# First feed-forward of a hybrid encoder layer: the first sequence's gate products taken from unnormalised rows, with 1/rms applied afterwards

## The chip, the core and the metric

The kernel runs on one core of a Trainium2 chip. Its engines have queues of their own and run in the order in which their instructions stand: PE (TensorE, matrix products, with its weight loads shown as PEld), DVE (VectorE), ACT (ScalarE), POOL (GpSimd) and SP (SyncE, here the issuer of most DMAs). They wait for each other by semaphores. The metric is the device time of one execution in microseconds (us).

## The reference, cut to what matters

Two sequences of 512 tokens (`x_prompt`, `x_sample`, 1024 channels) go through one encoder layer: a feed-forward, a mixing block and a second feed-forward. The change touches the first feed-forward alone:

```python
def rms_norm(x, g):
    y = xf * lax.rsqrt(jnp.mean(xf * xf, axis=-1, keepdims=True) + EPS)
    return (y * g.astype(jnp.float32)).astype(x.dtype)

def swiglu(x, w_gate, w_up, w_down):
    return (jax.nn.silu(x @ w_gate) * (x @ w_up)) @ w_down

x = x + 0.5 * swiglu(rms_norm(x, ffn1_norm), ffn1_w_gate, ffn1_w_up, ffn1_w_down)
```

All of it is float32; `D_FF` is 2816, so 22 blocks of 128 features.

## The kernel before

Activations lie with channels on the 128 partitions and tokens along the free dimension, so the token rows of the input are first transposed on PE (`turn`, L1236). Each float32 operand is split into a rounded half and a rest (`put`, L278 and L279, for activations; `w_pair`, L291 and L292, for weights), and `product` (L333) makes 12 matmuls of one product: four blocks of 128 channels by three pairings of halves.

Gate and up projections of both sequences are computed together by a scheme with seven products instead of eight (named B11, B21, B22, T1 to T4). B11 and B21 are the two channel halves of the plain gate product of the first sequence: after B11 its partial sum is copied out as `v1` (L341), after B21 the whole is copied out through Silu as `g0` (L348). The other five need sums of both sequences and of gate and up weights. This gives 22 steps, one for each block of features.

For ten of the 22 blocks, the products B11 and B21 are made ahead (`Up.begin`) while the second sequence is still being loaded, normalised and summed; `v1` and `g0` are parked in DRAM (`kept`) and fetched again in `resume` (L467). `Up.rest` then goes through all 22 steps in the order of `ORDER`, which alternates a resumed block (five products) with a fresh one (seven products), and ends on four fresh and two resumed blocks. `gu_rest` is one step: product T2 into bank Y, T1 into Z, T3 on top of Y, B22 on top of Z, T4 on top of Y. Between them DVE reads the banks: L364 adds `v1` and Y and must be done before T3 may write to Y; L372 reads Y before T4, L377 reads Z, L382 reads Y last. The results are split and written to DRAM by `Sides.out` (L396, L397) for the down projection.

At the start, SP issues the loads of the four token blocks of `x_prompt`, one of `x_sample`, the gate weights of block 0, then the rest. `rows_rstd` squares and sums each token row as its block lands and makes 1/rms by eleven small DVE instructions; `turn` transposes all four token blocks for one channel block at a time, each into a bank of its own; `keep_x` copies the turned rows out and stores them; `bcast_psum` (L213) spreads 1/rms over the partitions; `first_x` multiplies the turned rows by the norm weight and 1/rms (`scaled`, L1260) and splits them. Only then can `begin(0)` run. The norm weight `g1` and four small tensors of the mixing block are loaded by POOL's DMA queue, element by element.

A planner orders the instructions of each engine by program order and by the offsets given with `shifted`; `pin` keeps the written order.

Of the kernel before, what the change touches and what calls it, by code (L numbers as in the profile page):

```python
# [26 lines left out]
def encoder(ctx, tc, I, outs):  # L27
# [95 lines left out]
    nc.gpsimd.dma_start(g1, I["ffn1_norm"][0].rearrange("(k p) -> p k", p=P))  # L123


# [4 lines left out]
    pw = PT()[:, 0:P]  # L130
# [150 lines left out]
    def right_sums(xc, k, x0l, x0u, x1l, x1u):  # L281

        V_.tensor_tensor(x0l, x1l, x0l, op=ALU.subtract)
        V_.tensor_tensor(x1l, x1u, x1l, op=ALU.subtract)
        V_.tensor_tensor(x1u, x1u, x0l, op=ALU.subtract)
        V_.tensor_tensor(x0u, x0u, x1u, op=ALU.subtract)
        for i, t in ((T1, x0l), (T2_, x1u), (T3, x1l), (T4, x0u)):
            put(xc[i], k, t)

    def w_pair(t, src, pin=lambda i: i):  # L290
        pin(nc.scalar.activation(t[:, 0], src, AF.Copy))  # L291
        pin(V_.tensor_tensor(t[:, 1], src, f(t[:, 0]), op=ALU.subtract))  # L292
# [11 lines left out]
    def gu_left_a(rg, pin=lambda i: i):  # L304

        wa = w8_tile()
        w_pair(wa, rg.rearrange("p (a k) c -> p a k c", a=2), pin)
        return {B11: part(wa, 0), B21: part(wa, 1)}
# [34 lines left out]

    def gu_first_b(X, W, xc, g0):

        product(X, W[B21], xc[B21], False)
        with shifted(SOONER):
            nc.scalar.activation(g0, X, AF.Silu)  # L348

    def gu_rest(W, xc, got, ring, mid):  # L350
# [75 lines left out]
    class Up:  # L426


        def __init__(self, xc, wg, wu, rb):
            self.xc, self.rb = xc, rb  # L430
# [3 lines left out]
            self.ring.rows["o"] += tables(FFN_ROWS)  # L434
            self.ring.join("x", "v", "h")
# [14 lines left out]
        def begun(self):  # L450
            if self.open:
                j, X, W = self.open
                t = self.ring("k")
                gu_first_b(X, W, self.xc, t)
# [3 lines left out]
        def left(self, j):  # L458
            return gu_left_a(self.fetch(j, (0,))[0])

        def rest(self, raw, at=None, hook=None):
            ring = self.ring

            def resume(j):
                got = ring("v"), ring("h")
                for t, d in zip(got, self.kept.pop(j)):
                    nc.sync.dma_start(t, d)  # L467
                return got
# [5 lines left out]
            for i, j in enumerate(ORDER):  # L474
# [8 lines left out]
                h = gu_rest(W, self.xc, got, ring, lambda: then.append(resume(nxt)) if nxt in self.kept else None)  # L483
# [730 lines left out]
    pin = tc.keep_in_program_order  # L1214
    for _ in range(8):
        pin(nc.tensor.matmul(pw, ones, ones, start=True, stop=True))
# [7 lines left out]
    up = Up(xc, I["ffn1_w_gate"][0], I["ffn1_w_up"][0], rbuf[0])  # L1224
    xins = [I[n][0] for n in ("x_prompt", "x_sample")]

    kept = [[dpool.tile([P, S], F32, name=f"kept{j}_{i}") for i in range(2)] for j in range(AHEAD)]

# [4 lines left out]
    def turn(s, k, bank):  # L1233
        p = bank()
        for b in range(4):
            nc.tensor.transpose(p[:, b * P:(b + 1) * P], raws[s][:, b, k * P:(k + 1) * P], ident)  # L1236
        return p
# [6 lines left out]
    orow = up.ring.rows["o"]  # L1244

    def rows_rstd(s, engines):

        sq = [spool.tile([P, 4], F32, tag="cs4", bufs=4, name=nm("cs4")) for _ in range(2)]
        for b in range(4):
            for i in range(2):  # L1250
                x_, to = raws[s][:, b, i * S:(i + 1) * S], sq[i][:, b:b + 1]
                if engines[i] is V_:
                    V_.scalar_tensor_tensor(orow[3 + i], x_, 1.0, x_, op0=ALU.mult, op1=ALU.mult, accum_out=to)
                else:
                    nc.scalar.activation(orow[3 + i], x_, AF.Square, accum_out=to)
        V_.tensor_tensor(sq[0], sq[0], sq[1], op=ALU.add)
        return rstd_cols(sq[0], 4, D)
# [5 lines left out]
    raw0 = up.fetch(0, (0,), raws[0][:, 1, 0:1])  # L1263
    load_x(1)
    raw1 = [up.fetch(j, (0,))[0] for j in (1, 2)]
    x0 = up.ring.rows["x"]
    x0r = orow[:2] + up.ring.rows["s"] + orow[5:7] + orow[2:3]
    rs = rows_rstd(0, (V_, nc.scalar))
    for k, bank in enumerate((MM, PS, PT, MM, PS, PT, MM, PO)):
        keep_x(0, k, turn(0, k, bank), x0r[k])  # L1270
    W = [gu_left_a(raw0[0])]
    with shifted(-60):
        R0 = bcast_psum(rs)
# [6 lines left out]
    for k in range(HK_):  # L1280
        first_x(k)
    up.begin(0, W[0])
    W.append(gu_left_a(raw1[0]))
    for k in range(HK_, KD):
        first_x(k)
# [3 lines left out]
    rs = rows_rstd(1, (nc.scalar, nc.scalar))  # L1289
    raw0 += up.fetch(0, (1,))  # L1290
# [5 lines left out]
    for k in range(HK_):  # L1296
        x1l, x1u = x1[2 * k % 4], x1[(2 * k + 1) % 4]
        for t, kk, bank, kr in ((x1l, k, PS, orow[3]), (x1u, k + HK_, PT, orow[4])):
            p = turn(1, kk, bank)
# [220 lines left out]
```

## Time and profile before

| | |
|---|---|
| median of 3 runs | 2083.98 us (2081.9 to 2084.88) |
| the profiled execution's own time | 2082.11 us |
| its span, first to last instruction | 2080.3 us |
| granted clock of TensorE, mean | 0.997 |
| PE busy | 2060.4 us (99%) |
| DVE busy | 1551.1 us (75%) |
| ACT busy | 894.6 us (43%) |
| POOL busy | 97.7 us (5%) |

The profile has a page with busy times, a strip of 40 slices, queues and the costliest groups, and views of the trace: a timeline by engine (start, length, engine, line, operation, tile written and tiles read, count, and in brackets the idle time before and what ended it), groups by line, waits, and tables by stretch (length, busy time and count of PE, PEld, DVE, ACT and POOL, then the granted clock, the busy share of the DMA engines and GB/s). Consecutive instructions of a kind stand merged in one row, with their count. DVE and ACT instructions overlap a little at their ends, so that the distance between two starts is less than the length of one.

### The profile page before, as it was taken

To read this page: it belongs to the slowest core of one execution; us is meant where nothing else is said; L and a number is where in the kernel's file an instruction comes from. 1 tells how busy PE (TensorE), PEld (TensorE's weight loads), DVE (VectorE), ACT (ScalarE), POOL (GpSimd) and SP (SyncE) were. 2 spreads that over 40 slices of the span, in tenths; PEclk is the share of its full clock that TensorE was granted. 3 is DMA by queue.
4 is the path that set the end of the run, shared out by engine and by line. 5 is a ranking of instruction groups with operands and counts; after the bars stand their busy time and mean duration, and the time that the engine had idled before them with its cause. 6 is when DMAs were issued, how large, how long until landed. Compare 5 with 4: busy or idle time off the path is not lost.

```text
span 2080.3 us, 27215 instructions
## 1 busy us (share of the span) xinstructions
PE 2060.4 (99%) x9478; PEld 1691.4 (81%) x9478; DVE 1551.1 (75%) x2836; ACT 894.6 (43%) x1645; POOL 97.7 (5%) x114
## 2 busy tenths in 40 slices
PE   8999999999999999999999999999999999999998
PEld 6888888888888877888878788888888888888887
DVE  7888888786797897575567646555788888786797
ACT  6544444443234566463345443324444444442222
POOL 1000000001003000100120000002000000000000
PEclk9999999999999999999999999999999999999999
DMA  9655655599766655777684345677656555599753
GB/s 280 203 173 194 193 171 182 200 342 362 262 222 243 218 152 174 265 240 268 210 286 160 107 149 190 208 255 245 200 177 200 192 172 182 187 348 347 270 189 116
DMA packets 307065, 454.33 MB, mean 218 GB/s; under 512 B 20064, under 2 KB 178864, under 8 KB 305904
## 3 DMA queue, kind: packets, MB, share of 16 engines
q1 hardware_dynamic: 305056, 447.13, 63.6%
q0 software_dynamic: 1872, 5.46, 0.8%
q8 instruction: 75, 1.23, 0.2%
q14 instruction: 62, 0.51, 0.1%
HBM read 285.63 MB, written 166.89 MB: 218 GB/s over the span
## 4 chain that ended last, share of the span: by engine, by line
PE 95%; DVE 3%; DMA 1%; ACT 1%; issue 0%; SPq 0%; DVEq 0%; ACTq 0%
PE mm L755 20%; PE pss L333 17%; PE pst L333 11%; PE mm L333 10%; PE mm L589 9%; PE pst L589 4%; PE pss L589 4%; PE mm L739 4%; PE pso L589 3%; PE pso L1029 1%; PE pss L1002 1%; PE pso L739 1%; PE pst L1021 1%; PE pso L1165 1%; PE pst L755 1%; PE pss L755 1%
## 5 line engine op out<-in xcount | busy, mean ns | idle before, releaser
L755 PE MATMUL mm<-xh,w 128*128 128x512 f32 x896 | 290.4, 394 | 0.0
L333 PE MATMUL pss<-xc,w 128*128 128x512 f32 x1056 | 256.2, 391 | 0.6 <-DVE t L364 0.6
L333 PE MATMUL mm<-xc,w 128*128 128x512 f32 x1056 | 253.4, 391 | 2.0 <-DVE w L292 0.7
L333 PE MATMUL pst<-xc,w 128*128 128x512 f32 x1056 | 253.6, 389 | 0.0
L333 PEld LDWEIGHTS pss<-xc,w 128*128 128x128 f32 x1056 | 196.9, 188 | 47.8 <-DVE t L364 7.2
L333 PEld LDWEIGHTS mm<-xc,w 128*128 128x128 f32 x1056 | 197.3, 188 | 45.2 <-DVE w L292 1.4
L333 PEld LDWEIGHTS pst<-xc,w 128*128 128x128 f32 x1056 | 198.2, 188 | 41.2
L755 PEld LDWEIGHTS mm<-xh,w 128*128 128x128 f32 x896 | 167.7, 188 | 33.5
L589 PE MATMUL mm<-rt,w 128*128 128x512 f32 (+1 forms) x819 | 188.4, 384 | 0.0
L755 PE MATMUL mm<-xl,w 128*128 128x512 f32 x448 | 176.2, 393 | 0.0
L589 PEld LDWEIGHTS mm<-rt,w 128*128 128x128 f32 x819 | 151.3, 188 | 29.8
L291 ACT ACTIVATE w<-t 128x512 fp32r<-128x512 f32 x176 | 106.9, 627 | 139.0 <-issue 55.2
L292 DVE TENSOR_TENSOR w<-t,w 128x512 fp32r<-128x512 f32 x176 | 118.3, 689 | 54.9 <-ACT w L291 52.9
L333 PE MATMUL pss<-xc,f 128*128 128x512 f32 x528 | 126.8, 389 | 0.0
L333 PEld LDWEIGHTS pss<-xc,f 128*128 128x128 f32 x528 | 99.1, 188 | 20.6
L657 ACT ACTIVATE w<-wr 128x512 fp32r<-128x512 f32 x72 | 45.1, 632 | 138.2 <-PE pso L589 70.8
L657 ACT ACTIVATE w<-t 128x512 fp32r<-128x512 f32 x82 | 51.8, 632 | 107.4 <-PE pst L589 62.4
L755 PEld LDWEIGHTS mm<-xl,w 128*128 128x128 f32 x448 | 84.2, 188 | 16.6
L589 PE MATMUL pss<-rt,w 128*128 128x512 f32 x396 | 93.7, 389 | 0.0
L589 PE MATMUL pst<-rt,w 128*128 128x512 f32 x396 | 93.7, 389 | 0.0
L239 ACT ACTIVATE w<-wr 128x1024 fp32r<-128x1024 f32 (+1 forms) x56 | 57.3, 1028 | 73.7 <-PE mm L755 30.2
L589 PEld LDWEIGHTS pss<-rt,w 128*128 128x128 f32 x396 | 74.3, 188 | 15.4
(343 smaller groups left out, 3641.6 us busy)
## 6 DMA issues: line engine op xcount, KB each, us to landing
rt<-rbuf SPq DMA_DIRECT2D x154, 512.0 KB, 5.4
wpark<-w SPq DMA_DIRECT2D x104, 512.0 KB, 3.4
w<-wpark SPq DMA_DIRECT2D x104, 512.0 KB, 4.7
wr<-in_ffn_w_gate_dram SPq DMA_DIRECT2D x62, 512.0 KB, 5.3
rbuf<-tab SPq DMA_DIRECT2D x102, 256.0 KB, 4.0
wr<-in_ffn_w_up_dram SPq DMA_DIRECT2D x44, 512.0 KB, 4.6
rbuf<-f SPq DMA_DIRECT2D x72, 256.0 KB, 4.0
wr<-in_w_in_dram SPq DMA_DIRECT2D x36, 512.0 KB, 6.0
```

Of the source, the lines that this page charges most:

```text
L239: pin(nc.scalar.activation(hi, raw, AF.Copy))
L291: pin(nc.scalar.activation(t[:, 0], src, AF.Copy))
L292: pin(V_.tensor_tensor(t[:, 1], src, f(t[:, 0]), op=ALU.subtract))
L333: nc.tensor.matmul(p, a[:, k, :], xt[:, b, k, :], start=(first and k == 0 and i == 0), stop=(k == HK_ - 1 and i == 2), skip_group_check=True)
L589: nc.tensor.matmul(p, u[:, a, d * P:(d + 1) * P], r[:, b, ts], start=(first and q == 0 and k == 0), stop=(q == len(us) - 1 and k == 2), sk ...
L657: nc.scalar.activation(hi, src, AF.Copy)
L739: nc.tensor.matmul(p[b][:, :N], a[:, k, bs], w_[:, kl, :], start=(k == 0 and i == 0), stop=(k == KD - 1 and i == 2))
L755: nc.tensor.matmul(p, a[:, k, :], b, start=(k == 0 and i == 0), stop=(k == n - 1 and i == 2))
L1002: nc.tensor.matmul(p, qT[:, h, b * P:(b + 1) * P], kv[:, hk * 2 + j, :], start=(j == 0), stop=(j == 1))
L1021: nc.tensor.transpose(p[:, b * P:(b + 1) * P], Ps[b][:, kb * P:(kb + 1) * P], ident)
L1029: nc.tensor.matmul(po, Vst[:, kv_, hk, :], w, start=(kv_ == 0 and i == 0), stop=(kv_ == 3 and i == 1))
L1165: nc.tensor.matmul(po, vm[:, a, t, hs_], b, start=(t == 0 and n == 0), stop=(t == 3 and n == 2))
```

## The change

The first sequence's rows go into B11 and B21 with the norm weight alone. Since 1/rms belongs to a token, which is a column of the result, it can be applied to `v1` and `g0` later: `scale_first` does so on POOL, for the resumed blocks after they are fetched and for the fresh ones after they are copied out, with Silu behind it as an ACT instruction of its own. The unscaled rows are also kept in `x0` and multiplied by 1/rms later, for the sums with the second sequence. Besides:

- `x_prompt` is turned token block by token block, into six banks at once (two more channel blocks follow), with `busy` products of ones between them; the norm weight comes in as eight rows, by ACT's DMA queue, and is turned on PE;
- the gate weights of blocks 0 (in two halves) and 1 are issued ahead of `x_sample`;
- the first sequence's 1/rms leaves the way to `begin(0)`; the second sequence's is one `pow` on POOL, and half of its squares move from ACT to DVE;
- the rest half of the split of every second gate block ahead (`left(j, G_)`, four of them), of `xc[B22]` and of `xc[T3]` (four each) moves from DVE to POOL;
- the four small loads of the mixing block wait on POOL until `xc[T4]` has its first rows.

```diff
-    def w_pair(t, src, pin=lambda i: i):
+    def w_pair(t, src, lo=None, pin=lambda i: i):
         pin(nc.scalar.activation(t[:, 0], src, AF.Copy))
-        pin(V_.tensor_tensor(t[:, 1], src, f(t[:, 0]), op=ALU.subtract))
+        pin((lo or V_).tensor_tensor(t[:, 1], src, f(t[:, 0]), op=ALU.subtract))
...
+    def scale_first(row, v1, g0):
+        if v1 is not None:
+            G_.tensor_tensor(v1, v1, row, op=ALU.mult)
+        if g0 is not None:
+            G_.tensor_tensor(g0, g0, row, op=ALU.mult)
+            nc.scalar.activation(g0, g0, AF.Silu)
...
             X = gu_first_a(W, xc, v1)
+            if row is not None:
+                scale_first(row, v1, None)
             second()
-            gu_first_b(X, W, xc, g0)
+            gu_first_b(X, W, xc, g0, AF.Silu if row is None else AF.Copy)
+            if row is not None:
+                scale_first(row, None, g0)
...
                     nc.sync.dma_start(t, d)
+                if self.row is not None:
+                    scale_first(self.row, *got)
                 return got
...
         pin = tc.keep_in_program_order
+        late = f(up.xc[T4][:, 0, 0, :])
+        for t in (gm, g2, gbias, hn):
+            G_.tensor_copy(t, late[:, 0:t.shape[-1]])
...
-    for _ in range(8):
-        pin(nc.tensor.matmul(pw, ones, ones, start=True, stop=True))
...
+    def rows_rstd(sq, power=False):
+        if not power:
+            pin(V_.tensor_tensor(sq[0], sq[0], sq[1], op=ALU.add))
+            return rstd_cols(sq[0], 4, D)
+        nhalf, a = square_cols()
+        G_.memset(nhalf, -0.5)
+        V_.tensor_tensor(a, sq[0], sq[1], op=ALU.add)
+        V_.tensor_scalar(a, a, 1.0 / D, EPS, op0=ALU.mult, op1=ALU.add)
+        G_.tensor_tensor(a, a, nhalf, op=ALU.pow)
+        return a
...
+    busy(8)
+    banks = [b() for b in (PS, PS, PT)]
+    pg = PT()
+    nc.tensor.transpose(pg[:, 0:KD], g1row, ident[0:KD, 0:KD])
+    V_.tensor_copy(g1, pg[:, 0:KD])
+    banks += [b() for b in (MM, MM, PO)]
+    sq = square_cols()
+    for b in range(4):
+        for k, p in enumerate(banks):
+            pin(turn(0, k, b, p))
+        if b < 3:
+            busy(2)
+            squares(0, b, sq, (V_, nc.scalar), pin)
     xc[B11], xc[B21] = xc_tile(), xc_tile()
 
     def first_x(k):
-        scaled(x0[k], x0r[k], k, R0)
-        put(xc[B11 if k < HK_ else B21], k % HK_, x0[k])
+        t, kk, p, g = xc[B11 if k < HK_ else B21], k % HK_, banks[k], g1[:, k:k + 1]
+        pin(nc.scalar.activation(t[:, 0, kk, :], p, AF.Copy, scale=g))
+        pin(V_.scalar_tensor_tensor(t[:, 1, kk, :], p, g, f(t[:, 0, kk, :]), op0=ALU.mult, op1=ALU.subtract))
...
+    todo = iter(range(KD))
+    ahead = lambda: first_x(next(todo))
+    ahead()
+    W = [gu_left_a(raw0, None, pin, ahead)]
+    late_turn(PT)
+    ahead()
+    keep_x(0, 0, banks[0], x0[0])
+    late_turn(PS)
+    W.append(gu_left_a(raw1[0], None, pin))
+    for k in todo:
         first_x(k)
+    for k in range(1, 4):
+        keep_x(0, k, banks[k], x0[k])
+    squares(0, 3, sq, (V_, nc.scalar), pin)
+    rs = rows_rstd(sq)
+    for k in range(4, KD):
+        keep_x(0, k, banks[k], x0[k])
+    V_.tensor_copy(R0, bcast_psum(rs))
     up.begin(0, W[0])
...
+        for t, kk in ((x0[k], k), (x0[k + HK_], k + HK_)):
+            scaled(t, t, kk, R0)
         for j in ((3,), (4, 5), (6, 7), (8, 9))[k]:
-            up.begin(j, up.left(j))
-        put(xc[B22], k, x1u)
-        right_sums(xc, k, x0[k], x0[k + HK_], x1l, x1u)
+            up.begin(j, up.left(j, G_ if j % 2 else None))
+        put(xc[B22], k, x1u, G_)
+        right_sums(xc, k, x0[k], x0[k + HK_], x1l, x1u, G_)
```

More of the change, by code (lines that the diff above doesn't have):

```diff
@@ L129, in encoder @@
     nc.vector.memset(ones, 1.0)
-    pw = PT()[:, 0:P]
+    pw = MM()[:, 0:P]
     warm = cpool.tile([P, 1], F32, name="warm")
@@ L1231, in load_x, with turn, busy @@
             nc.sync.dma_start(raws[s][:, b, :], xins[s][b * P:(b + 1) * P, :])
[L1233 to L1237, printed above, removed]
+    def turn(s, k, b, p):
+        return nc.tensor.transpose(p[:, b * P:(b + 1) * P], raws[s][:, b, k * P:(k + 1) * P], ident)
+    def busy(n):
+        for _ in range(n):
+            pin(nc.tensor.matmul(pw, ones, ones, start=True, stop=True))
     def keep_x(s, k, p, xt):
@@ L1262, in encoder @@
     load_x(0)
-    raw0 = up.fetch(0, (0,), raws[0][:, 1, 0:1])
+    raw0 = wpool.tile([P, KD, P], F32, tag="wr", bufs=4, name=nm("wr"))
+    for a in range(2):
+        nc.sync.dma_start(half(raw0, a), half(up.v[0], a)[:, :, 0:P])
+    raw1 = up.fetch(1, (0,))
     load_x(1)
[L1265 to L1270, printed above, removed]
@@ L1288, in encoder @@
     up.begin(2, W[2])
-    rs = rows_rstd(1, (nc.scalar, nc.scalar))
-    raw0 += up.fetch(0, (1,))
+    sq = square_cols()
+    for b in range(4):
+        squares(1, b, sq, (V_, nc.scalar))
+    rs = rows_rstd(sq, True)
+    raw0 = [raw0] + up.fetch(0, (1,))
     R1 = orow[2]
```

83 lines of the change are left out of this document (47 added, 36 removed).

## The prediction

> **What bounds the kernel now.** I read the page first, then the table by stretch of the start, then the engines' timelines there and in the steady part of the steps.
>
> ```profile
> PE 2060.4 (99%) x9478; PEld 1691.4 (81%) x9478; DVE 1551.1 (75%) x2836; ACT 894.6 (43%) x1645; POOL 97.7 (5%) x114
> 5.00:10.00 5.00, 1.14 (x5) 0.73 (x5) 1.85 (x7) 1.93 (x6) 3.22 (x5) 0.84 1.00 310
> 10.00:15.00 5.00, 5.00 (x25) 4.63 (x24) 2.45 (x15) 4.31 (x12) 0.13 (x1) 0.50 1.12 255
> 15.00:85.00 70.00, 67.61 (x310) 53.82 (x308) 62.54 (x100) 49.41 (x90) 0.10 (x1) 1.00 0.83 264
> ```
>
> PE bounds the whole: a change gains only where PE waits or has nothing useful yet. The change leaves the products as they are, so what counts is when they start and whether another engine holds them up. Up to 17.75 PE only turns and idles, at half clock from 10 to 15. From 15 to 85 DVE is busy 62.5 of 70 us: the second engine near its limit.
>
> ```profile
> 7.76 0.33 PE L1236 MATMUL mm<-ident,raw 128*128 128x128 f32 x1 [1.70 <-DMA raw<-in_x_prompt_dram]
> 9.55 0.48 PE L1236 MATMUL mm<-ident,raw 128*128 128x128 f32 x1 [1.46 <-DMA raw<-in_x_prompt_dram]
> 17.75 0.50 PE L333 MATMUL mm<-xc,w 128*128 128x512 f32 x1 [0.47 <-ACT xc L278]
> 81.92 2.88 PE L333 MATMUL pst<-xc,w 128*128 128x512 f32 x12
> 85.42 3.02 PE L333 MATMUL pss<-xc,w 128*128 128x512 f32 x12 [0.62 <-DVE t L364]
> 15.07 1.40 DVE L1260 SCALAR_TENSOR_TENSOR t<-f,g,pst 128x512 f32<-128x512 f32 x2 [2.11 <-PE pst L213]
> 84.68 0.68 DVE L364 TENSOR_TENSOR t<-t,pss 128x512 f32<-128x512 f32 x1
> ```
>
> At 85.42 the first resumed step's T3 is held by L364, the one place where PE waits for DVE in the steps. So the start has two measures: PE's, from the first product at 17.75 to T3 at 85.42, and DVE's, from 15.07 to the end of L364 at 85.36.
>
> **The change part by part. PE's start.** The last prompt block lands at 9.55 and its first turn takes 0.48; then the bank is copied, half a weight block split, and the product starts.
>
> ```profile
> 10.22 0.58 ACT L1241 ACTIVATE f<-mm 128x512 f32<-128x512 f32 x1
> 68.36 0.64 ACT L291 ACTIVATE w<-t 128x512 fp32r<-128x512 f32 x1
> 34.05 0.60 PE L1236 MATMUL pst<-ident,raw 128*128 128x128 f32 x4
> 1.04 3.78 PE L1216 MATMUL pst<-ones 128*128 128x128 f32 x16 [1.04 <-DVE st L979]
> ```
>
> 9.55 + 0.48 + 0.58 + 0.64 = 11.25, against 17.75: 6.5 us earlier. The six turns (0.9 by the third row) and four passes of ones (16 take 3.78, so 0.95) of a block fit between landings. Half a weight block, half a token block's bytes, lands some 0.9 behind the last (token blocks come 1.8 apart: 7.76, 9.55), in time. The turns and ones also fill the idle stretch behind the clock of 0.50, so I cost the first matmuls at full clock; at half clock the first 12 would lose one product, 2.7 us (12 are 2.88 with their tail in the row of 81.92). The Trainium skill (TensorE: Matmul & The Clock Gate, What's actually happening) has the clock fall to half after an idle window of about 3.4 us; the row of 5 to 10 agrees, with 1.14 us of work and the clock then at 0.50. Nothing in the sum hangs on it.
>
> If PE were all, T3 would move from 85.42 to 78.9.
>
> **DVE's work.** Prices, from start to start:
>
> ```profile
> 5.79 0.69 DVE L1253 SCALAR_TENSOR_TENSOR R<-raw 128x512 f32<-128x512 f32 x1 [0.73 <-DMA raw<-in_x_prompt_dram]
> 10.81 0.17 DVE L171 TENSOR_SCALAR rs<-rs 128x4 int32<-128x4 int32 x1
> 11.02 0.17 DVE L173 TENSOR_SCALAR rs<-rs 128x4 int32<-128x4 int32 x1
> 37.05 0.75 DVE L1260 SCALAR_TENSOR_TENSOR t<-pst,g,R 128x512 f32<-128x512 f32 x1
> 37.72 0.69 DVE L283 TENSOR_TENSOR t<-t,t 128x512 f32<-128x512 f32 x1
> 57.62 1.23 DVE L292 TENSOR_TENSOR w<-wr,w 128x1024 fp32r<-128x1024 f32 x1
> 58.76 0.69 DVE L279 TENSOR_TENSOR xc<-t,xc 128x512 fp32r<-128x512 f32 x1
> 59.36 0.68 DVE L284 TENSOR_TENSOR t<-t,t 128x512 f32<-128x512 f32 x1
> ```
>
> A sum or rest half costs 0.60, a scaling 0.67, a weight's rest half 1.14, a square 0.70, a small one 0.20. From its first rest half on, DVE gains five squares (one of the prompt, four of the sample, +3.5), the copy of 1/rms over partitions (+0.6), the prompt's two small ones more than the sample's saved by `pow` (+0.4), and 16 scalings where there were 8 scalings and 8 rest halves (+0.5). It loses four weights (4 x 1.14 = 4.6) and eight rest halves (8 x 0.60 = 4.8). 62.5 + 5.0 - 9.4 = 58.1. It starts behind ACT's first copy, at 9.55 + 0.48 + 0.58 = 10.6. With the waits of before (70.3 from 15.07 to 85.36, less 62.5: 7.8) L364 ends at 10.6 + 58.1 + 7.8 = 76.5, earlier than PE needs it.
>
> **What POOL takes back.** The moved work runs on POOL: four weights, eight rest halves, and three scalings of fetched tiles before that L364. No POOL instruction of 1024 columns is in the trace; twice the shorter one bounds it above, once below, and I take twice, as DVE's nearly doubles.
>
> ```profile
> 614.33 1.29 POOL L156 TENSOR_TENSOR R<-R,f 128x512 f32<-128x512 f32 x1 [117.00 <-ACT f L155]
> 616.07 1.29 POOL L156 TENSOR_TENSOR R<-R,f 128x512 f32<-128x512 f32 x1 [0.44 <-ACT f L155]
> 617.58 1.47 POOL L156 TENSOR_TENSOR R<-R,f 128x512 f32<-128x512 f32 x1 [0.23 <-ACT f L155]
> 614.69 1.48 DVE L595 TENSOR_TENSOR xs<-xs,e 128x512 f32<-128x512 f32 x1
> 616.70 1.21 DVE L595 TENSOR_TENSOR xs<-xs,e 128x512 f32<-128x512 f32 x1
> 617.83 1.78 DVE L658 TENSOR_TENSOR w<-wr,w 128x512 fp32r<-128x512 f32 x1
> ```
>
> 4 x 2.58 + 11 x 1.29 = 24.5 us of POOL. The rows show what that does to a busy DVE: instructions with two SBUF inputs, 0.69 alone, last 1.48, 1.21 and 1.78 beside POOL, each until POOL's own is over and its 0.6 has run. Lost: 0.79 + 0.52 + 1.09 = 2.40 of POOL's 4.05 us, 59%. The worst single case is 1.09 of 1.47, 74%; the best is nothing, where POOL runs while DVE waits or reads a bank. I take 59%, for DVE is as dense in the start as here: 24.5 x 0.59 = 14.5. Some of it falls into the 7.8 us in which DVE waits anyway, between none and all; I take half, 3.9. L364 ends at 76.5 + 14.5 - 3.9 = 87.1 (bounds: below PE's 78.9, and 76.5 + 18.1 = 94.6), against 85.36: 1.7 us later. So the 6.5 us come back, and a little more, as PE's wait for DVE, at the latest in front of the first T3.
>
> **Added waits.** The second sequence's `pow` stands on POOL behind the first moved weight; PE's spreading of it stands ahead of eight matmuls and block 2's B21, which wait with it. The `pow` itself is between POOL's 0.23 and 1.29 below; with the weight's 2.58 ahead of it PE stands still between 0 and 3.9, I take 2, but DVE bounds later, so nothing more in the sum. The mixing loads now issue behind the last moved weight, whose split is the row of 63.02 today:
>
> ```profile
> 8.21 0.75 POOL L678 DMA_DIRECT2D hn<-in_mlstm_head_norm_dram  x1
> 63.02 1.23 DVE L292 TENSOR_TENSOR w<-wr,w 128x1024 fp32r<-128x1024 f32 x1 [0.57 <-ACT w L291]
> 14.87 0.23 POOL L679 TENSOR_SCALAR hn<-hn 128x4 f32<-128x4 f32 x1 [5.90 <-DMA hn<-in_mlstm_head_norm_dram]
> ```
>
> L679 waits 6.7 us after the issue; behind it on POOL stands T3's last rest half, which DVE's next use of that row waits for, ahead of L364. From the end of that weight it takes four issues (3.0 by the row), 6.7 in place of the last one's own 0.75, 0.2 and 1.3: 10.4. From there to the end of L364 DVE has eight instructions, 5.3. So it is hidden while the weight is split by 87.1 - 5.3 - 10.4 = 71.4; today it is by 64.3, and with POOL's 2.58 in place of 1.23 by 65.6. Each us beyond 71.4 makes L364 a us later. The norm weight's load by ACT's queue must land by 10; L679's 6.7 from an issue near 1 bounds it at 7.7: nothing. On SP the first sequence's eight stores now stand behind block 3's weights and ahead of block 4's, which is neutral.
>
> **The steps.** Each pair of a fresh and a resumed step gets four POOL scalings and two Silu.
>
> ```profile
> 192.45 0.88 SPq L467 DMA_DIRECT2D t<-kept  x2
> 195.44 0.58 ACT L341 ACTIVATE t<-mm 128x512 f32<-128x512 f32 x1
> 200.85 0.60 ACT L348 ACTIVATE t<-mm 128x512 f32<-128x512 f32 x1 [3.15 <-PE mm L333]
> 202.00 1.29 DVE L292 TENSOR_TENSOR w<-t,w 128x512 fp32r<-128x512 f32 x2 [1.89 <-ACT w L291]
> 205.15 1.23 DVE L292 TENSOR_TENSOR w<-wr,w 128x1024 fp32r<-128x1024 f32 x1 [1.13 <-ACT w L291]
> 209.01 0.69 DVE L377 TENSOR_TENSOR t<-t,pst 128x512 f32<-128x512 f32 x1 [1.30 <-PE pst L333]
> 216.60 0.68 DVE L364 TENSOR_TENSOR t<-t,pss 128x512 f32<-128x512 f32 x1
> 217.34 3.04 PE L333 MATMUL pss<-xc,w 128*128 128x512 f32 x12
> ```
>
> The resumed step's T3 (217.34) follows its L364 (216.60) with no room, and DVE is dense from 209.01 to there. But the scalings come earlier: fetched tiles some 3 us behind 192.45, fresh ones behind 195.44 and 200.85, all over by about 203. DVE then waits 1.89 + 1.13 + 1.30 = 4.3 us before 209.01, against 4 x 1.09 = 4.4 lost at worst and 3.0 at 59% of 1.29. Absorbed; if one slipped past 209.01 it would cost PE 1.09 in each of eight pairs, 8.7. I take a tenth, +0.9. ACT is under half busy; its Silu (0.6) stands ahead of copies with 2 us to spare.
>
> **Sum.** +1.7 + 0.9 = +2.6. The profiled execution (2082.11, span 2080.3 and 1.8 around it) becomes 2084.7; it lies 1.9 below the median of the runs, which becomes 2086.6. That is within about 0.2%, 4.2 us, which a measurement of this kernel cannot tell from no change.
>
> **The rivals.** All but (c) differ in the lost share p: T3 moves by 24.5p - 12.8. (a) The early start is kept: POOL's work falls into DVE's waits, p is under 0.35, and PE bounds, T3 at 78.9 to 81 (with the 2 us behind `pow`). For it: DVE's sum of 76.5 without POOL, and the 7.8 us in which DVE waits as it is. Against it: nearly all that DVE has left later, sums and rest halves, reads two SBUF tiles, the kind that the rows show stretched. -6.5 to -4.4 leaves 2078.5, partly within 0.2%.
>
> (b) Slower, by the hold alone: POOL shuts DVE's two-input instructions out for its whole length, and one of them always stands there. At 74% L364 ends at 76.5 + 18.1 - 3.9 = 90.7, 5.3 late, and DVE enters the steps with a backlog that lets one pair in three lose 1.09 (+2.9): 2092. It decides from p = 0.66 on, where the sum passes 4.2. For it: 617.83. Against it: 614.69 and 616.70, which met POOL part of the way through and lost only what was left of it (0.79 and 0.52). The Trainium skill (SBUF — State Buffer, SBUF: two separate sides) states an exclusive lock, held for the whole instruction by the one that starts first, against DVE's two-input instructions; by that rule 617.83 is the normal case and the outcome is this rival's.
>
> (c) The change doesn't do what it says: weights or turns land late and the first product stays near 17, with POOL's hold hidden as DVE is 9.4 us lighter: 2084.
>
> **How the numbers follow.** Forecast 38%, (b) 36%, (a) 24%, (c) 2%. The forecast's own range is 2081 to 2088. Faster by over 0.2% (below 2079.8): four fifths of (a), 0.19; slower (above 2088.1): (b), 0.36; the rest 0.45. The range reaches into (a), to 2078, and from (b) takes T3's bound of 94.6 (+9.2) with the tenth, 2094.
>
> **What would show it.** First product of `first_x` near 11.3 with the clock at 1.0; DVE's two-input instructions stretched beside POOL from 26 on; the first resumed T3 near 87, waiting for the add of `v1`; L364 of the resumed steps still right ahead of T3. It is wrong if that T3 comes before 82 or after 89, or if the pairs grow longer.

## The result and the profile after

| | before | after |
|---|---|---|
| median of six runs each | 2082.7 us (2081.3 to 2084.88) | 2090.3 us (2088.16 to 2091.11) |
| ratio, 95% interval | | 1.0035 (1.0025 to 1.0045) |
| the profiled execution | 2082.11 us, span 2080.3 | 2090.44 us, span 2088.7 |

The change makes the kernel 7.6 us slower: beyond the 0.2% that was called no change, and inside the range of the prediction (2078 to 2094). The prediction gave "no change" the largest chance (0.45) and "slower" 0.36; slower is what came. In the kernel after, the lines of the prediction have new numbers: L336 is the product (L333 before), L276 the rest half of an activation (L279), L289 that of a weight (L292), L344 and L351 ACT's copies of `v1` and `g0`, L378 the add ahead of T3 (L364), L386 the next reading of that bank (L372), L1290 the `pow`.

The busy times of the page, then the table by stretch (length, busy time and count of PE, PEld, DVE, ACT and POOL, clock, DMA share, GB/s):

```profile
PE 2064.2 (99%) x9491; PEld 1693.1 (81%) x9491; DVE 1594.4 (76%) x2824; ACT 907.2 (43%) x1660; POOL 190.8 (9%) x174
```

```profile
5.00:10.00 5.00, 4.69 (x38) 4.01 (x36) 2.35 (x7) 2.87 (x9) 0.00 (x0) 1.00 1.08 362
10.00:15.00 5.00, 4.20 (x16) 2.41 (x16) 4.72 (x8) 5.00 (x9) 0.00 (x0) 1.00 1.07 380
15.00:85.00 70.00, 60.56 (x262) 48.34 (x263) 60.34 (x87) 42.53 (x78) 32.19 (x25) 0.93 0.74 236
9.47:92.14 82.67, 72.12 (x311) 56.56 (x308) 72.53 (x102) 52.52 (x94) 33.63 (x26) 0.94 0.74 238
```

Up to 15 us everything is better: PE is busy where it idled, and the clock is at 1.00. From 15 to 85 PE has 60.6 us of work where it had 67.6, and POOL 32.2 where it had 0.1. PE's timeline tells where its time went:

```profile
10.01 2.49 PE L336 MATMUL mm<-xc,w 128*128 128x512 f32 x7 [0.31 <-ACT w L288]
32.25 1.12 PE L210 MATMUL pst<-ident,cs 128*128 128x128 f32 x4 [2.86 <-POOL cs L1290]
33.87 6.78 PE L336 MATMUL mm<-xc,w 128*128 128x512 f32 x20
75.59 3.01 PE L336 MATMUL mm<-xc,w 128*128 128x512 f32 x12 [1.83 <-ACT f L344]
82.47 4.58 PE L336 MATMUL mm<-xc,w 128*128 128x512 f32 x12 [3.87 <-ACT f L344]
92.33 2.92 PE L336 MATMUL pss<-xc,w 128*128 128x512 f32 x12
125.37 3.04 PE L336 MATMUL pss<-xc,w 128*128 128x512 f32 x12
224.13 3.06 PE L336 MATMUL pss<-xc,w 128*128 128x512 f32 x12
```

The first product starts at 10.01, 7.74 us earlier than before (17.75). The first resumed T3 starts at 92.33, 6.91 us later (85.42). In between PE waits 2.86 us for `pow` and 1.83 and 3.87 us for ACT, which cannot empty the bank of the next product, and behind the longest two of these waits it runs slowly (12 matmuls take 4.58 us, against 3.01 behind the wait of 1.83). The later resumed T3 rows at 125.37 and 224.13 are three pairs apart, 32.92 us each; before, 217.34 was 6.79 earlier than 224.13, so the steps are not longer. What is lost is lost ahead of the first T3.

DVE and POOL on their timelines in the same stretch:

```profile
40.34 2.78 DVE L276 TENSOR_TENSOR xc<-t,xc 128x512 fp32r<-128x512 f32 x1 [1.93 <-ACT xc L275]
52.95 2.88 DVE L283 TENSOR_TENSOR t<-t,tab 128x512 f32<-128x512 f32 x1
66.49 2.89 DVE L276 TENSOR_TENSOR xc<-t,xc 128x512 fp32r<-128x512 f32 x1
87.29 2.21 DVE L289 TENSOR_TENSOR w<-wr,w 128x1024 fp32r<-128x1024 f32 x1
91.46 0.68 DVE L378 TENSOR_TENSOR t<-t,pss 128x512 f32<-128x512 f32 x1
```

```profile
40.17 2.40 POOL L289 TENSOR_TENSOR w<-wr,w 128x1024 fp32r<-128x1024 f32 x1
52.44 2.84 POOL L289 TENSOR_TENSOR w<-wr,w 128x1024 fp32r<-128x1024 f32 x1
66.28 2.55 POOL L289 TENSOR_TENSOR w<-wr,w 128x1024 fp32r<-128x1024 f32 x1 [1.03 <-ACT w L288]
```

Each of these three weights on POOL has a DVE instruction beside it that reads two SBUF tiles, lasts 2.8 to 2.9 us in place of 0.68, and ends 0.55 us behind POOL's. Between 15 and 92 twelve instructions of DVE are stretched so, each measured against its length alone (0.68, 0.74 for a scaling, 1.22 for a weight): 0.89 + 2.10 + 0.44 + 1.09 + 1.04 + 2.20 + 1.11 + 1.10 + 2.21 + 0.69 + 1.08 + 0.99 = 14.9 us. L378 ends at 92.14 and T3 starts right behind it.

### The profile page after: what moved, and what is told of

Same layout as the page of the kernel before. It is cut to its first block, busy times and chain, and to the rows that moved or that the text cites. A ratio compares the mean times of both kernels' runs of the same rounds, so it can differ in the third digit from the quotient of the medians.

```text
span 2088.7 us, 27324 instructions
## 1 busy us (share of the span) xinstructions
PE 2064.2 (99%) x9491; PEld 1693.1 (81%) x9491; DVE 1594.4 (76%) x2824; ACT 907.2 (43%) x1660; POOL 190.8 (9%) x174
## 4 chain that ended last, share of the span: by engine, by line
PE 94%; DVE 2%; ACT 1%; DMA 1%; issue 0%; POOL 0%; SPq 0%; DVEq 0%; ACTq 0%; POOLq 0%
PE mm L777 20%; PE pss L336 17%; PE pst L336 11%; PE mm L336 10%; PE mm L608 9%; PE pst L608 4%; PE pss L608 4%; PE mm L761 4%; PE pso L608 3%; PE pso L1051 1%; PE pss L1024 1%; PE pso L761 1%; PE pst L1043 1%; PE pso L1187 1%; PE pss L777 1%; PE pst L777 1%
## 5 line engine op out<-in xcount | busy, mean ns | idle before, releaser
L336 PE MATMUL mm<-xc,w 128*128 128x512 f32 x1056 | 258.0, 395 | 7.4 <-ACT f L344 6.5
L336 PE MATMUL pss<-xc,w 128*128 128x512 f32 x1056 | 256.2, 391 | 0.0
L336 PE MATMUL pst<-xc,w 128*128 128x512 f32 x1056 | 253.6, 389 | 0.0
L336 PEld LDWEIGHTS mm<-xc,w 128*128 128x128 f32 x1056 | 199.5, 190 | 51.9 <-ACT f L344 8.2
L336 PEld LDWEIGHTS pss<-xc,w 128*128 128x128 f32 x1056 | 196.9, 188 | 46.9 <-DVE t L378 6.2
L336 PEld LDWEIGHTS pst<-xc,w 128*128 128x128 f32 x1056 | 198.2, 188 | 41.1
L289 DVE TENSOR_TENSOR w<-t,w 128x512 fp32r<-128x512 f32 x176 | 130.0, 755 | 36.6 <-ACT w L288 34.5
L336 PE MATMUL pss<-xc,f 128*128 128x512 f32 x528 | 127.0, 389 | 0.6 <-DVE t L386 0.6
L336 PEld LDWEIGHTS pss<-xc,f 128*128 128x128 f32 x528 | 99.0, 188 | 21.5 <-DVE t L386 1.0
L608 PEld LDWEIGHTS pst<-rt,w 128*128 128x128 f32 x396 | 74.3, 188 | 15.4
```

The lines of the kernel that those rows point to most:

```text
L289: pin((lo or V_).tensor_tensor(t[:, 1], src, f(t[:, 0]), op=ALU.subtract))
L336: nc.tensor.matmul(p, a[:, k, :], xt[:, b, k, :], start=(first and k == 0 and i == 0), stop=(k == HK_ - 1 and i == 2), skip_group_check=True)
L608: nc.tensor.matmul(p, u[:, a, d * P:(d + 1) * P], r[:, b, ts], start=(first and q == 0 and k == 0), stop=(q == len(us) - 1 and k == 2), sk ...
```

## The experiments

Theory A1 (A in the first expectations), that of the prediction: POOL's instructions shut DVE's two-input ones out, and DVE's lateness makes T3 late. Rivals: the late data and weight slots of the slower rest halves (A2), the `pow` (B), the stores of the parked tiles behind weight fetches on SP (C). Every kernel is the changed one with the edit shown; T3 is the start of the first resumed T3.

Each ratio is to the kernel before as it ran beside that kernel, so that ratios compare better than medians. The first product starts between 9.97 and 10.93 us in these profiles, so T3 differences under 1 us say little.

| kernel | median us | ratio to before, 95% | T3 | span |
|---|---|---|---|---|
| before (first profile) | 2082.7 to 2083.8 | 1 | 85.42 | 2080.3 |
| after | 2090.3 | 1.0035 (1.0025 to 1.0045) | 92.33 | 2088.7 |
| e1_no_hold | 2081.9 | 0.9989 (0.9981 to 0.9998) | 82.99 | 2080.1 |
| e2_no_pow | 2090.4 | 1.0035 (1.0022 to 1.0047) | 92.38 | 2089.8 |
| e3_no_hold_no_pow | 2084.1 | 1.0003 (0.9994 to 1.0012) | 86.98 | 2082.4 |
| e4_kept_queue | 2093.5 | 1.0051 (1.0037 to 1.0064) | 94.17 | 2091.7 |
| e5_weights_back | 2083.9 | 1.0005 (0.9996 to 1.0014) | 87.37 | 2082.1 |
| e6_puts_back | 2086.6 | 1.0020 (1.0011 to 1.0028) | 89.10 | 2084.8 |
| e7_hold_alone | 2091.4 | 1.0039 (1.0027 to 1.0052) | 93.45 | 2090.9 |
| e8_no_reads | 2085.4 | 1.0010 (1.0001 to 1.0019) | 87.03 | 2082.5 |
| e9_scale_dve | 2078.3 | 0.9978 (0.9969 to 0.9988) | 80.62 | 2075.8 |
| e10_rows_act | 2081.9 | 0.9993 (0.9984 to 1.0002) | 86.43 | 2082.1 |
| e11_fresh_bank | 2080.3 | 0.9986 (0.9977 to 0.9995) | 83.15 | 2079.4 |
| e12_kept_queue_early_loads | 2095.0 | 1.0056 (1.0042 to 1.0070) | 90.48 | 2093.3 |

**The moved rest halves back on DVE.**

```diff
-            up.begin(j, up.left(j, G_ if j % 2 else None))
-        put(xc[B22], k, x1u, G_)
-        right_sums(xc, k, x0[k], x0[k + HK_], x1l, x1u, G_)
+            up.begin(j, up.left(j))
+        put(xc[B22], k, x1u)
+        right_sums(xc, k, x0[k], x0[k + HK_], x1l, x1u)
```

> The changed kernel with every rest half of the start back on DVE (four weights, four of B22, four of T3: 9.4 us of DVE by the row prices); `pow` and the scalings stay on POOL. Theory A (POOL's rest halves hold DVE and free the weight slots late; the lateness comes back to PE as its waits of 1.83 and 3.87 us for ACT's copies and the half clock behind them, some 7.5 in all): those waits go or shrink under 2 in sum, the first resumed T3 comes at 84 to 87 instead of 92.3, time 2082 to 2085. Theory B (the `pow` on POOL is what costs): only what `pow` gains from having no weight ahead of it, T3 at 90 to 92, time 2088 to 2091. Theory C (stores of the parked tiles stand behind weight fetches on SP): the same waits stay, time 2088 to 2091.

T3 comes at 82.99, a little under the interval of A1, and the time is 2081.9: with 9.4 us more to do, DVE is done 9.2 us earlier. The table by stretch from DVE's first rest half to the end of L378:

```profile
9.74:82.93 73.19, 68.09 (x311) 53.09 (x308) 68.35 (x113) 52.30 (x93) 11.95 (x14) 1.00 0.82 265
```

Here DVE waits 73.19 - 68.35 = 4.8 us; in the changed kernel 82.67 - 72.53 = 10.1. PE's two waits for ACT are gone, and the clock stays at 1.00.

**Without `pow`.**

```diff
-    rs = rows_rstd(sq, True)
+    rs = rows_rstd(sq)
```

> The changed kernel with the second sequence's 1/rms made by the small DVE instructions as before, no `pow`; the moved rest halves stay on POOL. Theory A: PE's stall of 2.86 us and the half clock behind it (some 5 together) go, but PE then waits as much more for ACT's copies, as DVE's lateness is unchanged: T3 at 90.5 to 92.5, time 2088 to 2091. Theory B: T3 at 86 to 88, time 2084 to 2086.

> Both: all rest halves of the start on DVE and no `pow`; the early first product and the scalings on POOL stay. Theory A: as without the hold alone, or up to 3 us better where PE's stall was the rest of the loss: T3 at 81 to 86, time 2079 to 2084. Theory B: no better than without `pow` alone, 2084 to 2086. If DVE's own work bounds with nothing on POOL (9.4 us more than in the changed kernel), T3 at 87 or later, time 2085 or more.

The second of these two kernels has the edit of the first run as well. With the hold in place T3 stays where it was (92.38), though PE's wait for 1/rms shrinks from 2.86 to 1.24 us. PE's timeline shows the gain given back:

```profile
36.64 0.91 PE L210 MATMUL pst<-ident,rs 128*128 128x128 f32 x4 [1.24 <-DVE rs L189]
81.46 4.50 PE L336 MATMUL mm<-xc,w 128*128 128x512 f32 x12 [3.72 <-ACT f L344]
92.38 3.06 PE L336 MATMUL pss<-xc,w 128*128 128x512 f32 x12 [0.98 <-DVE t L378]
```

B falls. Without the hold, leaving `pow` out even costs 2.2 us: T3 is at 86.98, above the interval of A1 and just short of the 87 that was named for DVE's own work as the bound. The small instructions stand spread over DVE's queue, and the second sequence's 1/rms is spread over the partitions at 39.14 us, against 30.20 with `pow`. So, without the hold, `pow` is a useful part of the change.

**The stores of the parked tiles on ACT's queue**, and then also the mixing block's loads without the copies that hold them.

```diff
-            nc.sync.dma_start(kept[j][0], t)
+            nc.scalar.dma_start(kept[j][0], t)
...
-                nc.sync.dma_start(kept[j][1], t)
+                nc.scalar.dma_start(kept[j][1], t)
```

```diff
-        late = f(up.xc[T4][:, 0, 0, :])
-        for t in (gm, g2, gbias, hn):
-            G_.tensor_copy(t, late[:, 0:t.shape[-1]])
```

> The changed kernel with the stores of the parked tiles issued by ACT, right behind its copies, instead of by SP, where they stand behind weight fetches that wait for a slot. Theory A: ACT's waits for those stores (10.7 us from 15 to 93) go, but DVE stays late by POOL's hold: T3 at 89 to 92, time 2087 to 2090. Theory C: the waits of PE for ACT's copies go with them, T3 at 84 to 86, time 2082 to 2085.

> The changed kernel with the stores of the parked tiles issued by ACT, as in the fourth of these runs, and without the copies that hold the mixing block's loads until the last moved weight is split; there DVE waited 5.27 us for a rest half of T3 that stood on POOL behind the last of those loads. That wait goes: T3 at most 88.9 if nothing takes its place. Theory A1 (DVE is bound by its own 57.6 us of work, some 15 lost beside POOL and its waits of 7 to 10): T3 at 88 to 92, time 2087 to 2090. Theory C (the stores behind the weight fetches on SP carried the lateness to PE; DVE has room): T3 at 84 to 86, time 2082 to 2085.

The first of the two was slower than both theories had it, from another cause. In its timelines of POOL and then DVE:

```profile
66.09 2.94 POOL L289 TENSOR_TENSOR w<-wr,w 128x1024 fp32r<-128x1024 f32 x1 [3.67 <-ACT w L288]
...
78.99 0.24 POOL L701 TENSOR_SCALAR hn<-hn 128x4 f32<-128x4 f32 x1 [5.69 <-DMA hn<-in_mlstm_head_norm_dram]
79.21 1.25 POOL L276 TENSOR_TENSOR xc<-tab,xc 128x512 fp32r<-128x512 f32 x1
```

```profile
80.49 1.74 DVE L282 TENSOR_TENSOR tab<-tab,t 128x512 f32<-128x512 f32 x1 [5.27 <-POOL xc L276]
```

The last moved weight ends at 69.0, the load of `hn` behind it lands at 79, and T3's rest half and DVE wait for it: the chain that the prediction had worked out as 10.4 us from the weight to the end of that rest half, and that is hidden in the changed kernel. It takes 11.4 here. With the loads out of the way, T3 is at 90.48, inside the interval of A1 though above the 88.9 that held if nothing took the place of that wait. The stores do have a part: in the changed kernel ACT's timeline has, ahead of PE's waits of 1.83 and 3.87 us:

```profile
74.94 0.60 ACT L344 ACTIVATE f<-mm 128x512 f32<-128x512 f32 x1 [3.91 <-DMA kept<-f]
79.26 0.60 ACT L351 ACTIVATE f<-mm 128x512 f32<-128x512 f32 x1 [2.16 <-DMA kept<-f]
```

With these waits gone, ACT waits for DVE's sum instead (2.44 us ahead of PE's wait of 2.16), and PE waits another 1.67 us for L378. Stores and loads together give T3 1.9 us (2.8 counted from the first product, which starts at 10.93 here): C does not carry the loss. The time missed its interval, 2095.0, for the loads now issue in the middle of the steps. POOL, ACT and PE there:

```profile
311.27 0.24 POOL L698 TENSOR_SCALAR hn<-hn 128x4 f32<-128x4 f32 x1 [4.20 <-DMA hn<-in_mlstm_head_norm_dram]
311.49 1.26 POOL L357 TENSOR_TENSOR t<-t,tab 128x512 f32<-128x512 f32 x1
```

```profile
312.78 0.63 ACT L358 ACTIVATE t<-t 128x512 f32<-128x512 f32 x1 [5.79 <-POOL t L357]
```

```profile
313.94 4.61 PE L336 MATMUL pst<-xc,w 128*128 128x512 f32 x12 [3.81 <-ACT t L382]
```

A scaling stands on POOL behind the load, ACT's Silu waits for it, the copy of the next bank stands behind the Silu, and PE waits 3.81 us. With work on POOL in the steps, a wait of POOL for a load reached PE.

**Weights or activations alone.** Of the edit of the first run, the first line alone, and the other two alone.

> The changed kernel with the rest halves of the four gate blocks back on DVE; those of B22 and T3 stay on POOL. Theory A1 (what costs is the time for which POOL shuts DVE out): the rest halves of B22 and T3 were 12.4 of the moved 22.6 us of POOL, so some 55% of the 9.3 us between the changed kernel's T3 (92.3) and the one without moved rest halves (83.0) stay: T3 at 86 to 90, time 2085 to 2088. Theory A2 (what costs is the weight's slot, freed 1.3 us later by the slower split, and the fetch and stores behind it on SP): T3 at 83 to 85, time 2081 to 2084.

> The changed kernel with the rest halves of B22 and T3 back on DVE; those of the four gate blocks stay on POOL. Theory A1: 10.2 of 22.6 us of POOL remain, 45% of the loss: T3 at 85 to 89, time 2084 to 2087. Theory A2: nearly all of the loss remains: T3 at 89 to 92, time 2088 to 2091.

Of the 9.3 us between T3 with and without the moved rest halves (the two parts needn't add up to it), 4.4 stay with the activations' on POOL (forecast 55%, measured 47%) and 6.1 with the weights' (forecast 45%, measured 66%). T3 with the weights' on POOL (89.10) lies just above the interval of A1 and at the lower edge of that of A2; with the activations' (87.37) it lies in that of A1 and well above that of A2. Neither set alone is the cause, so A2, which put all on the weights, falls. The weights' larger share has a part of its own: PE waits 3.1 us for `pow` where the first moved weight stands ahead of it, and 1.5 us where it does not. The time of the first, 2083.9, is lower than A1 had it.

**The hold by itself, then POOL's work without reading.** DVE keeps all its rest halves; POOL works on a scratch row `dz` of 256 columns at the places where it had them, and nobody uses what it makes.

```diff
+    def hold(src, n):
+        G_.tensor_copy(dz[:, 0:1], src)
+        for _ in range(n):
+            G_.tensor_tensor(dz, dz, dz, op=ALU.mult)
...
-            up.begin(j, up.left(j, G_ if j % 2 else None))
-        put(xc[B22], k, x1u, G_)
-        right_sums(xc, k, x0[k], x0[k + HK_], x1l, x1u, G_)
+            Wj = up.left(j)
+            if j % 2:
+                hold(f(Wj[B11][0])[:, 0, 0:1], 3)
+            up.begin(j, Wj)
+        put(xc[B22], k, x1u)
+        hold(f(xc[B22][:, 0, k, 0:1]), 2)
+        right_sums(xc, k, x0[k], x0[k + HK_], x1l, x1u)
+        hold(f(xc[T3][:, 0, k, 0:1]), 2)
```

In the second of the two, two `G_.memset(dz, 0.5)` stand in place of the multiplication.

> All rest halves of the start on DVE, as in the first of these runs, and at the twelve places where the changed kernel had POOL make one, POOL multiplies a scratch row of 256 columns by itself instead (three times for a weight, twice for the others, some 0.75 us each, 21 us in all), started by one column of the same rounded half; nobody waits for the result. The order of instructions on PE, DVE and SP is the same as without them. Theory A1 (the hold alone): DVE loses 0.5 to 0.7 of each us that POOL works, some 10 to 14 us, and T3 comes at 90 to 97, time 2088 to 2096, though no data come from POOL any later. Theory A2 (late data and late slots): T3 at 83 to 85, time 2081 to 2084, as without them.

> As the run before it, but at each place POOL only writes the scratch row (two fills in place of one multiplication, about the same time); it reads one column to start. If what shuts DVE out is POOL's reading of SBUF, T3 stays at 83 to 85, time 2081 to 2084; if any work of POOL on SBUF does, T3 at 88 or later, time 2087 or more.

Idle work costs as much as the moved rest halves, though no rest half comes from POOL: T3 at 93.45 and 2091.4 us, 10.5 and 9.5 us more than without it. DVE's timeline beside three such multiplications, which take 2.99 us together from 46.56 on:

```profile
46.96 1.10 DVE L1304 SCALAR_TENSOR_TENSOR t<-t,g,tab 128x512 f32<-128x512 f32 x1
47.98 1.10 DVE L281 TENSOR_TENSOR t<-tab,t 128x512 f32<-128x512 f32 x1
49.00 1.10 DVE L276 TENSOR_TENSOR xc<-t,xc 128x512 fp32r<-128x512 f32 x1
```

DVE's instructions start 1.02 us apart, about the length of one of POOL's, so the two take turns here, and each DVE instruction is 0.36 to 0.42 us longer. Beside the fills of the other kernel DVE keeps its lengths:

```profile
53.67 1.22 DVE L289 TENSOR_TENSOR w<-wr,w 128x1024 fp32r<-128x1024 f32 x1
54.81 0.68 DVE L276 TENSOR_TENSOR xc<-t,xc 128x512 fp32r<-128x512 f32 x1
55.41 0.68 DVE L280 TENSOR_TENSOR t<-t,t 128x512 f32<-128x512 f32 x1
```

```profile
53.74 0.31 POOL L1256 MEMSET tab<- 128x256 f32 x1
54.11 0.31 POOL L1257 MEMSET tab<- 128x256 f32 x1
54.48 0.31 POOL L1256 MEMSET tab<- 128x256 f32 x1
```

T3 is nevertheless at 87.03 and the time 3.5 us above that without any of it: between the two forecasts (83 to 85, and 88 or later). ACT's timeline has the reason: the scalings of the fetched tiles stand on POOL behind the fills, and the split of T2's weight behind the Silu.

```profile
78.37 0.63 ACT L358 ACTIVATE t<-t 128x512 f32<-128x512 f32 x1 [3.87 <-POOL t L357]
```

PE and DVE wait 3.1 and 3.4 us for that weight. The idle multiplications have such a wait of PE too (3.80 us), so the 10.5 us by which they move T3 are not all DVE's. So what stretches DVE is POOL's reading, and not its being busy; this run alone does not give its price in time. The Trainium skill (SBUF — State Buffer, SBUF: two separate sides) has the lock against DVE's two-input instructions only where the GpSimd instruction reads SBUF; both runs agree, with 1.10 us against 0.68.

DVE's own account sorts this out. From its first rest half to the end of L378, in us: what its rows last beyond their length alone (stretched), what it is not busy (waits), and the rest (own work):

| kernel | own work | stretched | waits | L378 ends |
|---|---|---|---|---|
| after | 57.6 | 14.9 | 10.1 | 92.14 |
| e1_no_hold | 65.2 | 3.2 | 4.8 | 82.93 |
| e5_weights_back | 61.9 | 8.0 | 7.5 | 87.31 |
| e6_puts_back | 62.1 | 9.4 | 7.7 | 89.04 |
| e7_hold_alone | 65.3 | 11.8 | 5.0 | 91.57 |
| e8_no_reads | 65.4 | 0.8 | 9.2 | 85.16 |
| e9_scale_dve | 65.2 | 0.0 | 4.7 | 80.18 |
| e12_kept_queue_early_loads | 57.5 | 14.5 | 7.9 | 90.34 |

(e9_scale_dve, below, has no scaling on POOL either.) Idle work adds 8.6 us of stretch and next to no waiting, and L378 ends 8.6 us later. The moved rest halves take 7.6 us of work off DVE (9.4 by the prices, but two more rows of later work fall ahead of L378), add 11.7 us of stretch and 5.3 us of waits. So the hold by itself outweighs what the move saves by 4.1 us, and more than half of the loss is waiting, of which idle work made next to none: 2.6 us more than without moved rest halves with the activations' alone, 2.9 with the weights' alone. In that wider sense late data has a part in the loss; what each wait is made of stays open.

**The scalings on DVE as well**, then two more variants of that kernel.

```diff
         with shifted(SOONER):
-            nc.scalar.activation(v1, X, AF.Copy)
+            if row is None:
+                nc.scalar.activation(v1, X, AF.Copy)
+            else:
+                V_.tensor_tensor(v1, X, row, op=ALU.mult)
...
-            nc.scalar.activation(g0, X, func)
+            if row is None:
+                nc.scalar.activation(g0, X, func)
+            else:
+                V_.tensor_tensor(g0, X, row, op=ALU.mult)
+                nc.scalar.activation(g0, g0, AF.Silu)
...
     def scale_first(row, v1, g0):
-        if v1 is not None:
-            G_.tensor_tensor(v1, v1, row, op=ALU.mult)
-        if g0 is not None:
-            G_.tensor_tensor(g0, g0, row, op=ALU.mult)
-            nc.scalar.activation(g0, g0, AF.Silu)
+        V_.tensor_tensor(v1, v1, row, op=ALU.mult)
+        V_.tensor_tensor(g0, g0, row, op=ALU.mult)
+        nc.scalar.activation(g0, g0, AF.Silu)
```

(with the first run's edit; `row` is given for fresh blocks alone, and `scale_first` is left for the fetched ones). The second variant has the next two lines besides; in the third, `scale_first` stays on POOL.

```diff
-    V_.tensor_copy(R0, bcast_psum(rs))
+    nc.scalar.activation(R0, bcast_psum(rs), AF.Copy)
...
-    V_.tensor_copy(R1, bcast_psum(rs))
+    nc.scalar.activation(R1, bcast_psum(rs), AF.Copy)
```

> All rest halves of the start on DVE (the first of these runs, T3 at 83.0), and the scalings by 1/rms on DVE too: for fresh blocks straight out of the bank in place of ACT's copy, for fetched ones in place. Theory A1 (an instruction of POOL costs a busy DVE more than its own 0.60 us): the three POOL scalings ahead of the first T3 stretched DVE by 1.10, 1.04 and 1.10 us, 3.2 in all, against 3 x 0.60 = 1.8 of its own: T3 at 81 to 82.5. From 200 to 300 DVE's busy time falls from 96.7 to 90 to 93 (84.5 before the change, and 12 scalings of 0.60), and PE's waits of 1.0 us for L386 go: time 2079.5 to 2081.5. Rival (POOL's scalings were in DVE's waits and cost nothing): DVE's own 2.4 us of each pair come on top, T3 at 84 to 86 and busy time at 97 or more, time 2083 to 2086.

> As the run before it, and the two copies of 1/rms spread over the partitions go from DVE to ACT (1.2 us of DVE). DVE still bounds up to the first T3: T3 up to 1.2 earlier than in the run before it, 80 to 82, time 2078.5 to 2081. If ACT's copy comes late behind its other work, the second sequence's rows start later and T3 stays or moves back by up to 1: time 2080 to 2082.

> All rest halves of the start on DVE; fresh blocks are scaled by DVE straight out of the bank, fetched ones still by POOL. T3 stays at 83 as no fresh block is scaled ahead of it. By theory A1 DVE's busy time from 200 to 300 falls half as far as with both on DVE, to 93 to 95; pairs were not held up by it, so time 2081 to 2082.5, between the first of these runs and the one with both on DVE.

The first beats both kernels: 2078.3 us, 4.8 under before by the medians. T3 and the time lie a little below their intervals, DVE's busy time inside its own. T3 is at 80.62, and PE no longer waits for the add of `v1` (L378, L379 here):

```profile
80.62 2.88 PE L336 MATMUL pss<-xc,w 128*128 128x512 f32 x12
```

The table by stretch from 200 to 300 us, three pairs of steps, of the kernel before, of the changed one and of this one:

```profile
200.00:300.00 100.00, 100.00 (x439) 81.85 (x438) 84.53 (x133) 43.41 (x73) 0.00 (x0) 1.00 0.60 193
```

```profile
200.00:300.00 100.00, 100.00 (x439) 81.85 (x438) 96.67 (x135) 47.12 (x79) 18.00 (x12) 1.00 0.58 192
```

```profile
200.00:300.00 100.00, 100.00 (x439) 81.85 (x438) 91.88 (x146) 44.83 (x74) 0.00 (x0) 1.00 0.59 193
```

These stretches are a little longer than three pairs, and the second holds two instructions more than the first. Over exactly three pairs (98.8 us from one resumed T3 to the third next), DVE is busy 84.41, 95.49 and 91.00 us: twelve scalings on POOL cost DVE 11.1 us, 0.92 each; on DVE itself they cost 6.6 us, 0.55 each. PE was at 100 of 100 us in all three, so in the steps the difference costs no time but for PE's one wait for L386 (0.6 us at 405 in the changed kernel), which this kernel lacks. With only the fresh ones on DVE the time lies in between (2080.3), a little below its interval; its ratio cannot be told from that of e1_no_hold.

The copies of 1/rms on ACT were a miss: T3 at 86.43. PE's timeline:

```profile
33.76 1.12 PE L210 MATMUL pst<-ident,cs 128*128 128x128 f32 x4 [4.18 <-POOL cs L1291]
```

ACT's timeline shows why:

```profile
29.99 0.60 ACT L345 ACTIVATE f<-mm 128x512 f32<-128x512 f32 x1 [2.60 <-DMA kept<-f]
30.49 0.62 ACT L1278 ACTIVATE tab<-raw 128x512 f32<-128x512 f32 x1
```

In the order that the planner now wrote, the last square on ACT stands behind a copy that waits 2.60 us for the store of a parked tile; `pow` waits for the square, and PE for `pow`. The gain of 1.2 us on DVE was paid for with a longer wait of PE.

## Why the prediction was right and wrong, by its steps

- **PE's start.** Forecast 11.25, measured 10.01: the last token block was being turned at 8.39 already, not at 9.55. From that turn to the product it took 1.62 us against 1.70 in the sum. The clock was at 1.00, as taken.
- **DVE's work.** Forecast 58.1 us; measured 72.53 - 14.9 = 57.6. (The forecast took 62.5 us from the row of 15 to 85; from 15.07 to 85.36 DVE is busy 62.9, so its waits were 7.4 us and not 7.8. The sum of both stays.)
- **What POOL takes back.** Forecast 14.5 us lost, 59% of 24.5; measured 14.9. The size is right in part by luck: POOL's rest halves and scalings took 27.3 us, not 24.5, and DVE lost 55% of them. The mechanism is the one that the prediction had read from three rows, and the run with idle work on POOL shows it by itself.
- **What the waits absorb: here the step failed.** "Some of it falls into the 7.8 us in which DVE waits anyway, between none and all; I take half, 3.9", so that 3.9 us of waiting were to remain; 10.1 were measured. The sum against 87.1: 1.1 earlier start, 0.5 less work, 0.4 more lost, 6.2 more waiting, and L378 ends 5.0 later, at 92.14. The stall fell into no wait: with 0.0, 3.2 and 11.8 us of stretch (e9_scale_dve, e1_no_hold, e7_hold_alone) DVE waits 4.7, 4.8 and 5.0 us. The other 5.3 us of the changed kernel's waits came with the rest halves that POOL made. In three waits, 4.6 us together, DVE waits for ACT's rounded halves; ahead of two of them ACT had waited for the stores of the parked tiles (the rows of 74.94 and 79.26). One more, 1.2 us, is for a rest half of POOL's. That ACT's copies come late is also what PE waits for.
- **Where PE pays.** The prediction had PE wait for L378 in front of T3. PE waited 1.83 and 3.87 us earlier, for ACT, and then met L378 in time. That is another place for the same loss; putting the stores on another queue did not take it away. With the stores on ACT's queue, ACT waited for DVE in their place. How much of ACT's waiting each of its causes makes in the changed kernel stays open.
- **`pow`.** PE's 2.86 us lie within 0 to 3.9, though `pow` itself took 1.42, above the bound of 1.29; that it adds nothing to the sum is what the run without it shows.
- **The mixing block's loads.** The last moved weight ended at 68.83, ahead of the 71.4 given as the limit, and nothing was seen of them. The limit holds only for that forecast of DVE: with the other store queue the weight ended at 69.03, hardly later, but DVE came to T3's rest half at 75.2 and waited 5.27 us for it.
- **The steps.** Forecast +0.9. By T3 rows nothing is lost up to 399 us; then T3 goes from 6.8 to 7.7 us late by 440, with PE's one wait of 0.6 us for L386. The cause is of the kind that was forecast, a scaling on POOL beside a dense DVE (the kernel without scalings on POOL has no such wait), but it is one wait at another add, not a tenth of eight at L364: that the sizes agree is luck.
- **The sum.** +2.6 forecast; the profiled executions differ by 8.3: 6.9 ahead of T3, 0.8 in the steps, and 0.6 that no row explains and that lies within the scatter of the runs. T3 at 92.33 missed its own band (82 to 89), which the prediction had named as the sign of being wrong. The time lies outside the forecast's own range (2081 to 2088) and inside the stated one because that took in T3's bound of rival (b), not because the sum was right. Rival (b) came nearer to the number, 2092, by a lost share of 74% and by longer pairs, neither of which happened.

## What to carry to other kernels

Moving a two-input instruction from DVE to POOL gained nothing here where DVE was dense. A rest half of 512 columns saved DVE 0.60 us and stretched it by 0.6 (4.8 us for eight), a weight saved 1.14 and stretched it by 1.6 (6.2 us for four), and waits came on top; a scaling cost DVE 0.9 us on POOL and 0.55 on DVE itself. Count such a move as a loss unless POOL's part falls where DVE has nothing queued. When a stall is put into an engine whose waits are answers of other engines, do not let those waits absorb it: take none, and ask who waits for the engine that is now late. A slow kernel can hold a good idea: the rest of the change, the early start above all, is worth 4.8 us once the rest halves and scalings are back on DVE.

## What the runs showed of the hardware

- The hold works both ways: POOL's scaling, 1.26 to 1.30 us where undisturbed, means 1.5 us over the steps (18.00 us for 12). It took up to 3.42 us: at 353.65 in the changed kernel four DVE instructions, each 0.60 us behind the last, kept their 0.68 us, and POOL got no turn between them.
- `pow` on 128 x 4 took 1.41 to 1.50 us on POOL in every run that had it, a little more than an undisturbed multiplication of 128 x 512.
- The length of a wait of PE does not tell whether the clock falls. PE's rows behind a wait of 1.87 us (e12_kept_queue_early_loads) and behind one of 2.75 us (e6_puts_back):

```profile
30.87 3.81 PE L336 MATMUL mm<-xc,w 128*128 128x512 f32 x9 [1.87 <-ACT f L344]
```

```profile
78.25 3.06 PE L336 MATMUL mm<-xc,w 128*128 128x512 f32 x12 [2.75 <-ACT f L344]
```

Nine matmuls take 3.81 us behind the shorter wait, twelve take 3.06 behind the longer. The Trainium skill (TensorE: Matmul & The Clock Gate, What's actually happening) lets the clock fall after an idle window of about 3.4 us; here it fell behind a wait of little more than half of that, with work on PE up to it. In the kernel before, where the prediction saw the rule agree, no single wait ahead of the fall was longer than the 1.70 us of its row of 7.76. The same section calls the window free-running, so that the phase would decide; no run here shows the phase.
